# Spreading background steps, moving a DMA chain to GpSimd and re-ordering waits in a two-block transformer kernel

## Chip, cores and metric

One core of a Trainium2 chip runs the whole program. The metric is device microseconds of one execution, the median of several runs. The trace comes from one profiled execution, whose own time stands beside its span below.

## What is computed

Two model blocks of two layers each act on a sequence of 256 positions with 1024 channels. Layer 0 mixes by a state-space model (SSM) and by attention with 8 heads, layer 1 by a conformer convolution, layer 2 by latent attention (MLA) that also sees a context sequence, layer 3 by a Hyena convolution. After each mixer stands a gated feed-forward part. Each layer's norm is scaled and shifted by a modulation vector, a product of a conditioning vector with a large matrix. Cut to what matters:

```
for layer in range(DEPTH):                        # first block, DEPTH = 2
    mod = cs @ mod_w[layer] + mod_b[layer]        # 1024 x 6144
    sh1, sc1, g1, sh2, sc2, g2 = split(mod, 6)
    h = modulate(rms_norm(x, norm_g[layer, 0]), sh1, sc1)
    y = concat(s5_mixer(...), moba_attention(...)) @ ab_w_out   # layer 0
    y = conformer_conv(h, ...)                                  # layer 1
    x = x + g1 * y
    h = modulate(rms_norm(x, norm_g[layer, 1]), sh2, sc2)
    x = x + g2 * conv_ffn(h, ...)
x = rms_norm(x, final_g)
# second block: the same frame; layer 0 needs hc = modulate(rmsnorm(ctx), csh1, csc1)
# for the keys and values of the context, layer 1 is the Hyena mixer
```

## The kernel before

Activations lie channel by channel: eight tiles of 128 channels by 256 positions. All weights are float32 and are read once. A linear layer goes over blocks of 128 output channels (`linear`). For each block, `wsplit` takes a 512 KB load slot (`room`), loads the weights from the SP queue, lets ACT round them into `hi` (line 412) and DVE subtract to get `lo` (line 413); then `mm3` issues three matmuls per 128 input channels (lines 434 to 436), 24 for a block of 1024 inputs. The load slots are five tiles of the pool `raw`; in some stages `more` adds a second pool `raw2`, and `room` then takes the two pools in turn. `raw2` lies on memory that the stage before has used.

The language's planner orders each engine's instructions by a simulated time. `issue_after(ins)` in the program makes the instructions traced in it follow `ins` if they are on the same engine.

Modulation vectors are made in two ways beside the main work. `modulation` (lines 520 to 561) multiplies on PE, with the matrix as the moving operand: it loads four 512 KB tiles for each 512 outputs and yields after every second load; the products go into tile `mo`. `dotted_with` (line 498) makes 128 outputs per unit on DVE: GpSimd's queue loads 512 KB into `mraw` (line 504), and one DVE instruction (line 506) multiplies and sums. `later` and `also` put such work into lists, and `tick`, called after each block of `linear`, advances them: a counter `done` or `dotted` grows by one per block, and as often as it exceeds the step length, a step is issued. `need(layer)` issues all that is left up to a layer. `pace` sets the step length of the DVE units. The counters keep what they have when a list is empty (`done`) or when the pace changes (`dotted`).

A norm's scale is not known when the next stage begins. `Front` starts the first blocks of the next linear layer on unscaled data (`zh`, `zl`), twelve of them without a tick, while `stats` sums squares on PE, runs a Newton chain for the reciprocal root on DVE (`rsqrt`, lines 628 to 639) and spreads the result with two matmuls (`spread`, line 644). `stats2` does this twice in a row, for a norm behind a norm.

The SSM's lag kernels are built in `ssm_params`: a table `ktab` goes to DRAM (`kd`, line 992), and eight loads bring it back shifted (`kmat`, line 996). `ssm_out` (line 1073) uses `kmat` in its first matmuls (line 1089). `layer_ab` calls it after the first of four pairs of attention heads. In layer 1's feed-forward part `ffn1`, the function `context` runs between the last pair of gate and up blocks and the down blocks: it loads the context, norms it (`ctx_operand`) and makes its keys and values (`kv_latent`). In `layer_mla`, `positions` multiplies the rotary part `pe` of the keys (line 1423).

Of the kernel before, what the change touches and what calls it, by code (L numbers as in the profile page):

```python
# [11 lines left out]
F32 = mybir.dt.float32  # L12
# [265 lines left out]
class Front:  # L278
# [40 lines left out]

    def block(self, ps, wh, wl, evac):  # L320
# [4 lines left out]
        if self.n == 0 or self.n == self.spread:  # L325
            with net.tc.issue_after(net.last.ins):
                r = next(self.stats)
            if self.n:
                self.r = net.zp.tile([P, T], F32, name="zr")
                nc.scalar.activation(self.r, r, AF.Copy)  # L330
# [17 lines left out]
class Net:  # L348
    newton = 3

    def __init__(self, ctx, tc, d, where, dbg=None):
# [4 lines left out]
        self.turn = 0  # L356
# [81 lines left out]
    def linear(self, w, blocks, xh, xl, evac, n=T, acc=None):  # L438
# [132 lines left out]
    def pace(self, every):  # L571

        self.every = every
# [11 lines left out]
    def tick(self, n=1.0):  # L585
# [42 lines left out]
    def rsqrt(self, v):  # L628

        nc = self.nc  # L630
        y = self.t([P, 2], "ny")
        u = self.t([P, 2], "nu")
# [33 lines left out]
    def stats2(self, sq, sq2, r1):  # L666
# [101 lines left out]
    def down(self, w, hi, lo, evac, every=1.0):  # L768

        self.pace(every)  # L770
        self.linear(w, range(Front.late), hi, lo, evac)
# [4 lines left out]
    def ffn1(self, l, x, hi, lo, g2, sq, sq2=None, pool=None, mid=None, front=None):  # L776
        nc, d = self.nc, self.d
        with self.tc.tile_pool(name=f"ffn{l}", bufs=1, reuse_waits="tile") as fp:
# [19 lines left out]
            for j in range(FC):  # L798
                pair(j)
            if mid:  # L800
                mid()
            self.down(d[f"down{l}"], ah, al, self.residual(x, g2, sq, None, sq2, pool, front))
# [48 lines left out]
    def ssm_params(self, sp, spt):  # L851
# [265 lines left out]
    def layer_ab(self, x, hi, lo, g1, sq, sp, u2, vals, front):  # L1117
        nc, d = self.nc, self.d
        v = nc.vector
        with self.tc.tile_pool(name="ab", bufs=1, reuse_waits="tile") as ap, self.banks(mm=2, s=2, ax=1, o=1):  # L1120
# [23 lines left out]
            for c in range(4):  # L1144
# [3 lines left out]
                if c == 0:  # L1148
                    yc, yh, yl = self.ssm_out(sp, ap, u2)
# [230 lines left out]
    def ctx_operand(self, cxp, ch, cl, gc, sh):  # L1380
        nc, d = self.nc, self.d
        cx = []
        for k in range(0, DC, 4):
            raw = self.room().rearrange("p (k t) -> p k t", t=T)
            nc.sync.dma_start(raw, d["ctxT"][:, k : k + 4, :])
            cx += [raw[:, i, :] for i in range(4)]
        cq = []
        for k in range(DC):
            self.sumsq(cq, cx[k], k, DC, pool=cxp)
        r = self.rstd(cq, D)  # L1390
        for k in range(DC):
            t = self.t([P, T], "n2", pool=cxp)
            nc.vector.scalar_tensor_tensor(t, cx[k], gc[:, k : k + 1], r, op0=ALU.mult, op1=ALU.mult)
            nc.scalar.activation(ch[:, k, :], t, AF.Identity, bias=sh[:, k : k + 1])
            nc.vector.scalar_tensor_tensor(cl[:, k, :], t, sh[:, k : k + 1], ch[:, k, :].bitcast(F32),
                                           op0=ALU.add, op1=ALU.subtract)

    def layer_mla(self, x, hi, lo, g1, sq, ckh, ckl, pe, final, front):
        nc, d = self.nc, self.d
        v = nc.vector  # L1400
        with self.tc.tile_pool(name="mla", bufs=1, reuse_waits="tile") as mp:
# [18 lines left out]
            def positions(half):  # L1420
                s = slice(half * T, half * T + T)
                kp = self.ring("o")[:, s]
                nc.tensor.matmul(kp, self.rsum[:64, :], pe[:64, s], start=True, stop=True)
# [115 lines left out]
    def hy_filters(self, fp, hp, H):  # L1539
# [37 lines left out]
        for n in range(2):  # L1577
            ps = self.ax()
            nc.tensor.matmul(ps[:, :T], w, cur, start=True, stop=True)
            a = fp.tile([P, T], F32, name="fa", tag="fa")  # L1580
# [116 lines left out]
    def run(self, out):  # L1697
# [15 lines left out]
        with self.tc.tile_pool(name="sp", bufs=1, reuse_waits="tile") as sp:  # L1713
# [76 lines left out]
        next(cm)  # L1790
# [6 lines left out]
        self.ffn1(0, x, f, None, six(0, 5), sq, mid=mid, front=f2)  # L1797
# [3 lines left out]
        self.later(5, self.modulation(2, range(4), ("c_2", "c_ctx_2"), (mods[2], modc)), 5.0)  # L1801
# [12 lines left out]
        with self.tc.tile_pool(name="lat", bufs=1, reuse_waits="tile") as lat:  # L1814
# [8 lines left out]
            with self.tc.tile_pool(name="cx", bufs=1, reuse_waits="tile") as cxp:  # L1823

                def context():
                    ch = self.zp.tile([P, DC, T], F32R, name="ch", tag="zh")
# [88 lines left out]
```

## Time and profile before

| | us |
|---|---|
| median of 3 runs | 1523.81 (1521.16 to 1525.88) |
| the profiled execution's own time | 1522.47 |
| its span, first to last instruction | 1520.7 |
| PE busy | 1379.3 (91%) |
| PE weight loads busy | 1249.7 (82%) |
| DVE busy | 1195.9 (79%) |
| ACT busy | 839.3 (55%) |
| mean granted TensorE clock | 0.959 |

PE is TensorE's matmuls, DVE the vector engine, ACT the scalar engine, POOL GpSimd, SP the engine that issues most DMAs. L412 is line 412 of the kernel. A matmul that the clock grants half speed counts as busy for twice as long, so busy time is not all work. Times within the span count from its start.

### The profile page before, as it was taken

Reading aid. Unit: us, or ns where it says so; the run is one execution under the profiler, and the core shown is the slowest. Engines: PE = TensorE matmul, PEld = TensorE weight load, DVE = VectorE, ACT = ScalarE, POOL = GpSimd, SP = SyncE. Lnnn points to the kernel's source line nnn. Section 1 sums busy time; section 2 is a strip of 40 time slices with the busy share of each in tenths; the row PEclk is TensorE's granted clock in tenths of the full one; section 3 lists DMA queues with packets and bytes.
Section 4 is the critical chain, followed back from the end, with each engine's and each line's share of the span. In section 5 each row is a group of like instructions: output and inputs, shape, how many; then the busy total and the mean of one; then the engine's idle time right before and its main releaser. Section 6 shows DMA issues by size and latency. Waiting matters only on the chain.

```text
span 1520.7 us, 28172 instructions
## 1 busy us (share of the span) xinstructions
PE 1379.3 (91%) x10686; PEld 1249.7 (82%) x10686; DVE 1195.9 (79%) x2428; ACT 839.3 (55%) x1562; POOL 125.1 (8%) x166
## 2 busy tenths in 40 slices
PE   6969879999988689989987998989999999889997
PEld 3638779999973689989986877989998678889997
DVE  7958869978674678787968876899886979799954
ACT  5416466554452467554545765766545654676642
POOL 1000100101000000000100651000010000000000
PEclk9969989999999799998988999999999999999998
DMA  9476766878669246775835243467695664556651
GB/s 363 167 160 211 240 233 212 286 250 303 237 231 364 76 156 187 237 240 187 321 90 186 84 140 124 143 200 249 213 353 181 247 237 138 164 167 211 205 171 39
DMA packets 96214, 311.89 MB, mean 205 GB/s; under 512 B 14533, under 2 KB 18222, under 8 KB 95950
## 3 DMA queue, kind: packets, MB, share of 16 engines
q1 hardware_dynamic: 77054, 244.01, 48.7%
q0 software_dynamic: 17856, 65.02, 13.1%
q8 instruction: 84, 1.38, 0.4%
q10 hardware_dynamic: 1168, 1.06, 0.3%
q14 instruction: 52, 0.43, 0.1%
HBM read 308.73 MB, written 1.32 MB: 204 GB/s over the span
## 4 chain that ended last, share of the span: by engine, by line
PE 59%; issue 27%; DVE 6%; DMA 4%; ACT 2%; POOL 1%; SPq 0%; DVEq 0%; POOLq 0%; ACTq 0%
PE mm L434 16%; PE mm L436 16%; PE mm L435 16%; DVE lo L413 2%; PE o L1512 1%; POOL mraw L504 1%; DMA raw<-gate 1%; PE mo L532 1%; ACT hi L412 1%; PE ax L1612 1%; DMA kmat<-kd 1%; DVE mraw L506 1%; PE sx L1496 0%; PE s L434 0%; PE ax L1496 0%
## 5 line engine op out<-in xcount | busy, mean ns | idle before, releaser
L412 ACT ACTIVATE hi<-raw 128x1024 fp32r<-128x1024 f32 (+3 forms) x402 | 403.7, 1008 | 406.0 <-PE mm L435 285.3
L413 DVE TENSOR_TENSOR lo<-raw,hi 128x1024 fp32r<-128x1024 f32 (+3 forms) x402 | 465.3, 1161 | 167.0 <-ACT hi L412 161.8
L434 PE MATMUL mm<-hh,hi 128*128 128x256 f32 x1472 | 416.9, 287 | 16.4 <-DVE e L758 5.6
L436 PE MATMUL mm<-hh,lo 128*128 128x256 f32 x1472 | 415.5, 283 | 3.0 <-DVE lo L413 3.0
L435 PE MATMUL mm<-hl,hi 128*128 128x256 f32 x1472 | 414.9, 283 | 0.5 <-DVE hl L712 0.5
L434 PEld LDWEIGHTS mm<-hh,hi 128*128 128x128 f32 x1472 | 278.2, 190 | 26.0 <-issue 6.9
L435 PEld LDWEIGHTS mm<-hl,hi 128*128 128x128 f32 x1472 | 280.0, 190 | 5.1 <-DVE hl L712 2.0
L436 PEld LDWEIGHTS mm<-hh,lo 128*128 128x128 f32 x1472 | 279.8, 190 | 4.7 <-DVE lo L413 3.8
L434 PE MATMUL mm<-ah,hi 128*128 128x256 f32 x704 | 200.8, 286 | 1.5 <-ACT hi L412 1.5
L436 PE MATMUL mm<-ah,lo 128*128 128x256 f32 x704 | 198.6, 284 | 3.8 <-DVE lo L413 3.8
L435 PE MATMUL mm<-al,hi 128*128 128x256 f32 x704 | 198.3, 282 | 0.0
L434 PE MATMUL mm<-zh,hi 128*128 128x258 f32 x608 | 176.4, 295 | 20.6 <-ACT hi L412 10.9
L436 PE MATMUL mm<-zh,lo 128*128 128x258 f32 x608 | 176.2, 291 | 2.3 <-DVE lo L413 2.3
L435 PE MATMUL mm<-zl,hi 128*128 128x258 f32 x608 | 176.2, 291 | 0.0
L504 POOL DMA_DIRECT2D mraw<-modt x124 | 65.7, 530 | 1230.1 <-DVE mraw L506 1111.1
L506 DVE SCALAR_TENSOR_TENSOR mraw<-mraw,crow 128x1024 f32<-128x1024 f32 x124 | 149.9, 1219 | 6.3 <-DMA mraw<-modt 6.2
L434 PEld LDWEIGHTS mm<-zh,hi 128*128 128x128 f32 x608 | 118.9, 197 | 23.2 <-ACT hi L412 11.7
L436 PEld LDWEIGHTS mm<-ah,lo 128*128 128x128 f32 x704 | 132.6, 189 | 4.8 <-DVE lo L413 4.4
L434 PEld LDWEIGHTS mm<-ah,hi 128*128 128x128 f32 x704 | 133.3, 189 | 3.1 <-ACT hi L412 1.9
L435 PEld LDWEIGHTS mm<-al,hi 128*128 128x128 f32 x704 | 133.4, 190 | 1.0 <-issue 1.0
L436 PEld LDWEIGHTS mm<-zh,lo 128*128 128x128 f32 x608 | 119.7, 197 | 2.9 <-DVE lo L413 2.9
L435 PEld LDWEIGHTS mm<-zl,hi 128*128 128x128 f32 x608 | 120.6, 199 | 0.0
(416 smaller groups left out, 2076.4 us busy)
## 6 DMA issues: line engine op xcount, KB each, us to landing
raw<-up SPq DMA_DIRECT2D x132, 512.0 KB, 4.0
mraw<-modt POOLq DMA_DIRECT2D x124, 512.0 KB, 5.2
raw<-down SPq DMA_DIRECT2D x64, 512.0 KB, 4.6
raw<-mod SPq DMA_DIRECT2D x60, 512.0 KB, 6.2
raw<-gate SPq DMA_DIRECT2D x44, 512.0 KB, 4.7
raw<-down SPq DMA_DIRECT2D x32, 384.0 KB, 3.5
raw<-hy_in SPq DMA_DIRECT2D x24, 512.0 KB, 6.8
raw<-cm_in SPq DMA_DIRECT2D x16, 512.0 KB, 5.5
```

The source lines that it names most:

```text
L412: nc.scalar.activation(hi, src, AF.Copy)
L413: return nc.vector.tensor_tensor(lo, src, hi.bitcast(F32), op=ALU.subtract)
L434: nc.tensor.matmul(out, wh, xh, start=start, stop=False)
L435: nc.tensor.matmul(out, wh, xl, start=False, stop=False)
L436: self.last = nc.tensor.matmul(out, wl, xh, start=False, stop=stop)
L504: nc.gpsimd.dma_start(w, self.d[f"modt{layer}"][u])
L506: nc.vector.scalar_tensor_tensor(w, w, 1.0, row, op0=ALU.mult, op1=ALU.mult, accum_out=out[:, u : u + 1]))
L532: nc.tensor.matmul(acc[g * 32 : g * 32 + 32, :], wt, src, start=(g not in begun), stop=last)
L1512: nc.tensor.matmul(o[i * 64 : i * 64 + 64], vals[:, k, c : c + 64], pt[i][:, k, :], start=(k == 0), stop=(k == 3))
L1612: nc.tensor.matmul(ps, m[:, k, m0 : m0 + P], src[:, k, s], start=(k == 0), stop=(k == 1))
```

## The change

It has these parts:

- `tick` sets `done` to zero when no modulation step is left, and `pace` sets `dotted` to zero; in layer 1 of the first block the step length of the modulation on PE for layer 2 goes from 5.0 to 2.0. In layer 0 one more block of 512 outputs is made on PE (`range(4, 7)`), and DVE makes 12 units where it made 16, at pace 1.0 where it was 1.2.
- `kd` and `kmat` are issued from GpSimd's queue, and `ssm_out` follows the second pair of heads, behind the last matmul traced.
- The context's norm runs in three steps, before pairs 15, 17 and 18 of the feed-forward part, and the steps of `kv_latent` run behind the down blocks.
- `stats2` computes both reciprocal roots in one chain on four columns.
- The first five loads after `more` take slots of `raw`. The convolution filter's loads are issued before pair 8 and no longer at the stage's start.
- In `Front`, the weight splits of blocks 3 and 4 follow the Newton chain on DVE. `positions` follows the last matmul traced. One Hyena tile comes from another pool.

```diff
+    def guard(self):
+        return self.net.tc.issue_after(self.chain.ins) if self.n in (3, 4) else nullcontext()
...
     def room(self):
+        if self.hold:
+            self.hold -= 1
+            return self.raw.tile([P, 1024], F32, name="raw")
...
                 if front.first():
-                    front.block(ps, *self.wsplit(w[mb]), partial(evac, mb))
+                    with front.guard():
+                        wh, wl = self.wsplit(w[mb])
+                    front.block(ps, wh, wl, partial(evac, mb))
...
     def pace(self, every):
-        self.every = every
+        self.every, self.dotted = every, 0.0
...
             self.step()
+        if not self.pending:
+            self.done = 0.0
...
-        v1 = self.t([P, 2], "nv")
-        v.tensor_scalar(v1, st[:, 0:2], 1.0 / D, EPS, op0=ALU.mult, op1=ALU.add)
-        y1 = self.rsqrt(v1)
-        v2 = self.t([P, 2], "nv")
-        v.tensor_tensor(v2, y1, y1, op=ALU.mult)
-        v.tensor_tensor(v2, v2, st[:, 2:4], op=ALU.mult)
-        v.tensor_scalar(v2, v2, 1.0 / D, EPS, op0=ALU.mult, op1=ALU.add)
-        y2 = self.rsqrt(v2)
-        v.tensor_tensor(y2, y2, y1, op=ALU.mult)
+        a = self.t([P, 4], "nv4")
+        v.tensor_scalar(a[:, :2], st[:, 0:2], 1.0 / D, EPS, op0=ALU.mult, op1=ALU.add)
+        v.tensor_scalar(a[:, 2:], st[:, 2:4], 1.0 / D, None, op0=ALU.mult)
+        v.scalar_tensor_tensor(a[:, 2:], a[:, :2], EPS, a[:, 2:], op0=ALU.mult, op1=ALU.add)
+        y = self.rsqrt(a, 4)
+        y1, y2 = y[:, :2], y[:, 2:]
...
     def more(self, bufs):
             self.raws.append((p, "raw2"))
+            self.hold = 5
...
+    def down(self, w, hi, lo, evac, every=1.0, then=None):
+        for m in range(Front.late):
+            self.linear(w, [m], hi, lo, evac)
+            if then:
+                self.behind(then)
...
-            nc.sync.dma_start(kd[:, q, :, :].rearrange("s h m -> h s m"), kt[q * 32 : q * 32 + 16, :, :])
+            nc.gpsimd.dma_start(kd[:, q, :, :].rearrange("s h m -> h s m"), kt[q * 32 : q * 32 + 16, :, :])
...
-            nc.sync.dma_start(kmat[j * 16 : j * 16 + 16, :, j * 16 :],
+            nc.gpsimd.dma_start(kmat[j * 16 : j * 16 + 16, :, j * 16 :],
...
-                if c == 0:
-                    yc, yh, yl = self.ssm_out(sp, ap, u2)
+                if c == 1:
+                    with self.tc.issue_after(self.last.ins):
+                        yc, yh, yl = self.ssm_out(sp, ap, u2)
...
-            self.later(0, self.modulation(0, range(4, 6), cs, mods[:1]), 1.5)
+            self.later(0, self.modulation(0, range(4, 7), cs, mods[:1]), 1.5)
-            self.pace(1.2)
-            self.also(1, 0, 24, 40, row, mods[0])
+            self.pace(1.0)
+            self.also(1, 0, 28, 40, row, mods[0])
...
-        next(cm)
-        self.ffn1(0, x, f, None, six(0, 5), sq, mid=mid, front=f2)
+        self.ffn1(0, x, f, None, six(0, 5), sq, mid=mid, front=f2, at={8: lambda: next(cm)})
...
-        self.later(5, self.modulation(2, range(4), ("c_2", "c_ctx_2"), (mods[2], modc)), 5.0)
+        self.later(5, self.modulation(2, range(4), ("c_2", "c_ctx_2"), (mods[2], modc)), 2.0)
...
-                    self.ffn1(1, x, f, None, six(1, 5), sq, sq2, lat, context, f2)
+                    self.ffn1(1, x, f, None, six(1, 5), sq, sq2, lat, context, f2, {j: lambda: next(ctx) for j in (15, 17, 18)}, latent)
```

## Rows read from the trace of the kernel before

**Rows 1.** The page: span, and PE's busy time

```profile
span 1520.7 us, 28172 instructions
PE 1379.3 (91%) x10686; PEld 1249.7 (82%) x10686; DVE 1195.9 (79%) x2428; ACT 839.3 (55%) x1562; POOL 125.1 (8%) x166
```

**Rows 2.** PE's waits by releaser: us in total, times, longest

```profile
PE sx L644 <- DVE ny L638: 18.6, 6, 6.2
PE sx L1089 <- DMA kmat<-kd: 15.0, 1, 15.0
PE mm L434 <- ACT hi L412: 14.3, 8, 9.8
...
PE o L1423 <- DVE pe L1370: 4.5, 1, 4.5
...
PE sx L644 <- DVE ny L681: 3.4, 1, 3.4
```

**Rows 3.** Busy time by stretch: length, engines, granted clock, DMA share, GB/s

```profile
85.70:100.60 14.90, 0.00 (x0) 0.00 (x0) 8.73 (x33) 0.00 (x0) 0.00 (x0) 0.57 1.13 131
100.70:111.80 11.10, 11.10 (x113) 6.32 (x114) 3.03 (x3) 3.66 (x4) 0.00 (x0) 0.50 0.83 295
85.70:186.60 100.90, 83.18 (x728) 67.44 (x728) 73.93 (x177) 45.36 (x97) 7.40 (x14) 0.88 0.77 217
...
186.60:207.80 21.20, 9.43 (x59) 8.72 (x59) 10.56 (x21) 8.31 (x16) 2.36 (x4) 0.76 0.79 284
442.60:476.50 33.90, 25.45 (x125) 5.03 (x124) 5.81 (x19) 5.48 (x15) 1.05 (x2) 1.00 0.99 384
...
678.00:692.00 14.00, 6.65 (x28) 6.25 (x29) 10.01 (x31) 6.47 (x12) 0.00 (x0) 0.64 0.41 141
...
778.70:791.00 12.30, 6.41 (x28) 6.15 (x29) 8.22 (x23) 5.46 (x15) 0.00 (x0) 0.59 0.12 39
805.80:818.40 12.60, 6.25 (x22) 5.01 (x23) 8.81 (x37) 4.08 (x11) 0.53 (x1) 0.59 0.48 181
...
600.00:680.00 80.00, 78.00 (x659) 77.91 (x657) 64.45 (x110) 47.61 (x78) 4.22 (x8) 1.00 0.75 241
```

**Rows 4.** SP's queue in order of time, 60 to 100 us: start, length, issue

```profile
62.67 0.33 SPq L542 DMA_DIRECT2D raw<-mod  x1
82.59 1.77 SPq L992 DMA_DIRECT2D kd<-ktab  x4
87.15 8.25 SPq L996 DMA_DIRECT2D kmat<-kd  x8
...
97.64 0.35 SPq L425 DMA_DIRECT2D raw<-ab_in  x1
```

**Rows 5.** SP's queue in order of time, 170 to 212 us

```profile
171.34 10.49 SPq L425 DMA_DIRECT2D raw<-up  x5
...
187.47 0.43 SPq L425 DMA_DIRECT2D raw<-gate  x1
```

**Rows 6.** PE in order of time, 442 to 453 us: modulation products

```profile
442.57 4.50 PE L532 MATMUL mo<-raw,cs 128*32 128x512 f32 x40
...
448.74 1.05 PE L532 MATMUL mo<-raw,cs 128*32 128x512 f32 x4 [1.30 <-DMA raw<-mod]
```

**Rows 7.** DVE in order of time, 551 to 560 us: a Newton chain

```profile
551.61 0.16 DVE L653 TENSOR_SCALAR nv<-sx 128x2 f32<-128x2 f32 x1 [2.44 <-PE sx L624]
...
557.06 1.22 DVE L413 TENSOR_TENSOR lo<-raw,hi 128x1024 fp32r<-128x1024 f32 x1 [0.30 <-ACT hi L412]
558.21 0.15 DVE L638 SCALAR_TENSOR_TENSOR ny<-nu,ny 128x2 f32<-128x2 f32 x1
```

**Rows 8.** DVE in order of time, 799 to 811 us: a modulation unit

```profile
807.93 1.23 DVE L506 SCALAR_TENSOR_TENSOR mraw<-mraw,crow 128x1024 f32<-128x1024 f32 x1 [1.78 <-DMA mraw<-modt]
```

**Rows 9.** The page's DMA issues: count, KB each, median us to landing

```profile
mraw<-modt POOLq DMA_DIRECT2D x124, 512.0 KB, 5.2
...
raw<-gate SPq DMA_DIRECT2D x44, 512.0 KB, 4.7
```

More of the change, by code (lines that the diff above doesn't have):

```diff
@@ L327, in block @@
                 r = next(self.stats)
+                if self.n == 0:
+                    self.chain = net.chain
             if self.n:
@@ L355, in __init__ @@
         self.dbg = dbg or {}
-        self.turn = 0
+        self.turn = self.hold = 0
         self.ahead = False
@@ L626, in sums, with rsqrt @@
         return last
-    def rsqrt(self, v):
+    def rsqrt(self, v, n=2):
         nc = self.nc
-        y = self.t([P, 2], "ny")
-        u = self.t([P, 2], "nu")
+        y, u = (self.t([P, n], nm + (str(n) if n > 2 else "")) for nm in ("ny", "nu"))
         nc.vector.tensor_scalar(u.bitcast(I32), v.bitcast(I32), 1, None, op0=ALU.logical_shift_right)
@@ L764, in more, with ffn1 @@
             self.raws.append((p, "raw2"))
+            self.hold = 5
             yield
             self.raws.pop()
-    def down(self, w, hi, lo, evac, every=1.0):
+    def down(self, w, hi, lo, evac, every=1.0, then=None):
         self.pace(every)
-        self.linear(w, range(Front.late), hi, lo, evac)
+        for m in range(Front.late):
+            self.linear(w, [m], hi, lo, evac)
+            if then:
+                self.behind(then)
         self.pace(1000.0)
         self.linear(w, range(Front.late, DC), hi, lo, evac)
-    def ffn1(self, l, x, hi, lo, g2, sq, sq2=None, pool=None, mid=None, front=None):
+    def ffn1(self, l, x, hi, lo, g2, sq, sq2=None, pool=None, mid=None, front=None, at={}, then=None):
         nc, d = self.nc, self.d
@@ L798, in ffn1 @@
             for j in range(FC):
+                if j in at:
+                    at[j]()
                 pair(j)
@@ L801, in ffn1 @@
                 mid()
-            self.down(d[f"down{l}"], ah, al, self.residual(x, g2, sq, None, sq2, pool, front))
+            self.down(d[f"down{l}"], ah, al, self.residual(x, g2, sq, None, sq2, pool, front), then=then)
     def ffn2(self, l, x, hi, lo, g2, sq, mid, front=None):
@@ L1378, in kv_latent, with ctx_operand @@
         yield
-    def ctx_operand(self, cxp, ch, cl, gc, sh):
+    def ctx_operand(self, cxp, ch, cl, modc):
         nc, d = self.nc, self.d
+        self.need(5)
+        g = self.gain("a2c", modc[:, 8:16], self.par("norm_mix_g_2", 0, 8))
+        sh = modc[:, 0:8]
         cx = []
@@ L1386, in ctx_operand @@
             cx += [raw[:, i, :] for i in range(4)]
+        yield
         cq = []
@@ L1389, in ctx_operand @@
             self.sumsq(cq, cx[k], k, DC, pool=cxp)
-        r = self.rstd(cq, D)
+        stats = self.stats(cq, D)
+        self.behind(stats)
+        yield
+        with self.tc.issue_after(self.last.ins):
+            r = next(stats)
         for k in range(DC):
             t = self.t([P, T], "n2", pool=cxp)
-            nc.vector.scalar_tensor_tensor(t, cx[k], gc[:, k : k + 1], r, op0=ALU.mult, op1=ALU.mult)
+            nc.vector.scalar_tensor_tensor(t, cx[k], g[:, k : k + 1], r, op0=ALU.mult, op1=ALU.mult)
             nc.scalar.activation(ch[:, k, :], t, AF.Identity, bias=sh[:, k : k + 1])
@@ L1422, in positions @@
                 kp = self.ring("o")[:, s]
-                nc.tensor.matmul(kp, self.rsum[:64, :], pe[:64, s], start=True, stop=True)
+                with self.tc.issue_after(self.last.ins):
+                    nc.tensor.matmul(kp, self.rsum[:64, :], pe[:64, s], start=True, stop=True)
                 for i in range(4):
@@ L1579, in hy_filters @@
             nc.tensor.matmul(ps[:, :T], w, cur, start=True, stop=True)
-            a = fp.tile([P, T], F32, name="fa", tag="fa")
+            a = self.t([P, T], "e")
             v.tensor_scalar(a, ps[:, :T], self.par("hy_f", 2 * n), self.par("hy_f", 2 * n + 1), op0=ALU.add, op1=ALU.mult)
@@ L1823, in run @@
             with self.tc.tile_pool(name="cx", bufs=1, reuse_waits="tile") as cxp:
+                ch, cl = (self.zp.tile([P, DC, T], F32R, name=n, tag=t) for n, t in (("ch", "zh"), ("cl", "zl")))
+                ctx = self.ctx_operand(cxp, ch, cl, modc)
+                latent = self.kv_latent(ch, cl, ckh, ckl, pe, 0, kv0, cxp, self.ax)
                 def context():
-                    ch = self.zp.tile([P, DC, T], F32R, name="ch", tag="zh")
-                    cl = self.zp.tile([P, DC, T], F32R, name="cl", tag="zl")
                     self.need(6)
@@ L1831, in context @@
                     self.also(7, 2, 24, 40, row2[0], mods[2])
-                    gc = self.gain("a2c", modc[:, 8:16], self.par("norm_mix_g_2", 0, 8))
-                    self.ctx_operand(cxp, ch, cl, gc, modc[:, 0:8])
-                    for _ in self.kv_latent(ch, cl, ckh, ckl, pe, 0, kv0, cxp, self.ax):
-                        pass
+                    next(latent)
+                    self.behind(latent)
                 def gain():
```

1 line of the change is left out of this document (added).

## The prediction

> **What bounds the kernel now.** First the page: of a span of 1520.7 us PE is busy for 1379.3 [rows 1], so at most 141 us can be won by closing PE's idle time, plus what PE loses at half clock. Second PE's waits [rows 2]: the reader is to see that a few long waits carry much of it, one of 15.0 us on the lag kernels, one of 9.8 on a weight split, six on Newton chains, 18.6 in all. Third the stretches around those waits and around every place where DMA is near its top [rows 3]; there the reader sees idle PE and the granted clock: after the 15 us wait PE works 11.1 us at 0.50, the lower of its two levels (1.2 GHz), so a wait costs its own length and then half of the work behind it. In the long feed-forward stretches PE is busy for 78.0 of 80 us [rows 3]; nothing is to be won there, and whatever the change adds to PE there is paid in full.
>
> **Part A, lag kernels and state-space output.** SP's queue shows the cause [rows 4]: after a load at 62.67 it issues nothing until `kd` at 82.59, then eight `kmat` loads at 87.15, and the attention weights behind them only at 97.64. PE stands from 85.7 to 100.6 and then works 11.1 us at half clock: 14.9 + 5.6 = 20.5 us is the most that can go. The edit takes twelve issues from SP, so the weights come early and PE has the next query and key blocks to do. What is late next: DVE, busy for 73.9 of the stage's 100.9 us, less four units of 1.23 [rows 8], 69; and PE, 83.2 less 5.6 of slow clock, plus the added modulation block, four loads at 0.45 (below), 79.4. Both fit in 80 us, but PE now has less to put beside the first heads' softmax, because `ssm_out` comes a pair later. How long twelve small-row DMAs take on GpSimd no row shows. On SP the eight issues took 8.25 us and ended with the landing at 100.6; for equal loads of 512 KB GpSimd's take 5.2 and SP's 4.7 [rows 9]. The bounds are a gain of 20.5 and none; nearest is the wait's own row, and I take **13**. Behind them on GpSimd stand only `mraw` loads; three of these lie in their slots already, so DVE's first three units don't wait.
>
> The Trainium skill, SBUF — State Buffer, section "SBUF: two separate sides", says against this part that GpSimd cannot write descriptors for its DMAs while DVE runs an instruction in a mode with two ports. In the idle stretch DVE is busy for 8.73 of 14.9 us [rows 3], so by that rule, at most, `kmat` lands 8.7 us later and the gain falls to some 4; no row shows a GpSimd issue held in this way.
>
> **Part B, first feed-forward stage.** Before the stage ends SP loads five up tiles, and the first gate tile only at 187.47 [rows 5], since slots alternate and `raw2` becomes free with the stage. PE is busy for 9.43 of 21.2 us, at a clock of 0.76 [rows 3]: 11.8 idle and some 2 at half clock. With five held slots gate and up tiles of blocks 0 to 4 are there in time, five blocks of 24 matmuls; 659 in 80 us of the full stretch [rows 3] make 0.121 each, so five blocks are 14.5 us, an estimate, three times a load's 4.7 us [rows 9], and that covers the second pool's first landings. The four units fewer and the pace of 1.0 also take units and 512 KB loads off the stage's end, and the filter's loads move to pair 8, where PE is full and DMA is not. What is left is the last residual and its scaled copy on DVE and ACT, about 2 us. Bounds 3 and 13.7; I take **11**.
>
> **Part C, the burst in the convolution layer.** `done` grew during the whole feed-forward part, so the first tick issues all 14 steps at once: 12 + 16 = 28 loads. From 442.6 to 476.5 DMA is at 0.99 and PE busy for 25.45 of 33.9 us [rows 3]. Where the loads had landed, 40 rows, which are ten loads, took 4.50 us, 0.45 a load; where PE followed the loads, one took 1.05 [rows 6], as fewer products run side by side. Set to zero, the counter gives two loads per step: one step in the four blocks that tick, three in `fill` calls where PE is idle in any case, two under the output blocks, eight in the next feed-forward part. Six loads are hidden, 22 cost 0.45 to 0.53, 10 to 11.7 us. Of the stretch stay some 2 us of transposes. 33.9 - 2 - 11 = 21; I take **20**, bounds 10 and 22. The price is elsewhere: eight steps, 8.4 MB, come into the feed-forward part at 241 GB/s [rows 3]. In the 50 to 59 us that the steps take there, 12.1 + 8.4 = 20.5 MB need 53 us at the burst's 384 GB/s. That just fits: **1 us lost**, bounds 0 and 8. In the Hyena layer the same reset spreads 16 loads; PE is full there, so 0, with 3 either way.
>
> **Part D, the context.** From 678 to 692 PE is busy for 6.65 us at a clock of 0.64 [rows 3]: 7.4 idle, with the 6.2 us wait for a Newton chain [rows 2] in it, and up to 3.3 of half clock. The chain, the scaling and the context's blocks now lie beside the last pairs, where DVE is busy for 64.45 of 80 us; of the 10.0 us that DVE works in the first stretch most move there, which finds room in seven pairs (41 us) but not in one. I take **8**, bounds 2 and 10.7.
>
> **Part E, guard.** (18.6 - 6.2) / 5 = 2.5 us is each other wait on a Newton chain; three of the five are at a `Front`. The chain of 12 short instructions takes from 551.61 to 558.36, with four `lo` of 1.2 us in between [rows 7]. Two of them now come behind it; the chain ends some 2.3 earlier. But block 3 may then wait for its own `lo`, 1.2. I take 1.5 at each of three places, **4.5**, bounds 7.5 gained and 3.7 lost.
>
> **Part F, latent attention.** `stats2` saves 13 of 27 chain instructions, 13 x 0.16 = 2.1 [rows 7], and its guard two `lo`: the 3.4 us wait [rows 2] goes. Later PE waits 4.5 for `pe` [rows 2], because DVE stands behind units whose loads have not landed [rows 8]: `dotted` came in full from the stage before, and the reset ends that burst; besides, `positions` no longer overtakes the blocks before it. Both waits are followed by work at half clock, 0.59 over stretches with 6.41 and 6.25 busy [rows 3], up to 3.1 us each. 3.4 + 4.5 + 6.2 = 14.1 at most, none at least; I take **9**.
>
> **Sum.** 13 + 11 + 20 - 1 + 8 + 4.5 + 9 = 64.5. The profiled execution took 1522.5, 1.8 more than its span and 1.3 less than the median of 1523.8. 1522.5 - 64.5 = 1458; with the 1.3, **1459 us**.
>
> **Rivals.** (1) *A wait takes the place of the one removed*: `kmat` lands so late that PE, in order, stands at `ssm_out` as long as before. For it speaks that all small rows pass one issuing engine; against, that two more blocks of PE work and a softmax lie ahead of it. A is 0: 1472. (2) *The modulation loads meet DMA's limit* in the feed-forward part, 53 of at most 59 us: C gains 10 and costs 8: 1476. (3) *The change doesn't do what it says*: the planner keeps its simulated order, and since the edges bind one engine only, E and F bring nothing: 1459 + 13.5 = 1472.5. (4) *Slower*: the twelve DMAs crawl on GpSimd. The other parts gain 51.5; PE would have to stand at `ssm_out` for more than 14.9 + 51.5 = 66 us, that is `kmat` has to land after about 152 us, which is 69 us for twelve DMAs from 83 on, 5.8 each in a row. Then the units' loads behind them on GpSimd hold DVE too. From there it is slower than before, 1530 at 76 us of standing. Against it: a GpSimd load of 512 KB takes 5.2 us with its landing and several are in flight at a time.
>
> **How the numbers follow.** The forecast, 1440 to 1470, gets 0.53; (1) 0.15, (2) 0.13, (3) 0.11, (4) 0.04; a further 0.04 is for many parts at their low ends, 1500 to 1524. All upper bounds together, with 1 us for DMA left out, would give 1523.8 - 90 = 1434; I cut this at 1440, and on the other side go to 1492, past two rivals at once (1459 + 13 + 17 = 1489). A measurement of this kernel can tell 0.3%, 4.6 us, from no change. Faster: all of the forecast and of (1) to (3) and a little of the rest, 0.93; same 0.03; slower 0.04.
>
> **What would show it.** After the change PE's waits should have no entry for `kmat` above a few us, `ab_in` issues on SP should follow 63 us by some us, a gate tile should be issued before the stage's end, no stretch should have `mo` rows for more than 3 us in a row in the convolution layer, and the wait of 6.2 us, that of 3.4 and that of 4.5 should be gone. DMA in the second feed-forward part should rise to 300 GB/s or more with PE still full. The prediction is wrong if PE waits in that part for weights, if `ssm_out`'s first matmul waits over 10 us, or if the removed waits come back at the same places under another releaser.

## The result and the profile after

The changed kernel takes **1453.8 us** (median of 4 runs, 1450.3 to 1456.3), beside 1524.2 for the kernel before: a ratio of 0.954, with a 95% interval of 0.951 to 0.956, so 70 us are gone. The forecast was 1459, its range 1440 to 1492. The total is right; several of its terms are not, and that they cancel is luck, as the rest shows.

The page of the changed kernel: the span, and the engines' busy time.

```profile
span 1452.8 us, 28167 instructions
PE 1360.5 (94%) x10702; PEld 1239.5 (85%) x10702; DVE 1184.8 (82%) x2407; ACT 840.0 (58%) x1562; POOL 130.9 (9%) x174
```

PE's busy time fell by 19 us against [rows 1], and the span by 68: 49 us of the gain are idle time of PE. The mean granted clock rose from 0.959 to 0.973, so that less of the busy time is work at half clock. PE's waits by releaser (total, times, longest) show what is left.

```profile
PE mo L543 <- DVE s_den L923: 9.9, 1, 9.9
PE sx L656 <- DVE ny L650: 6.7, 3, 2.5
PE mm L443 <- ACT hi L418: 6.4, 5, 3.6
PE mm L443 <- DVE qk L419: 5.1, 1, 5.1
PE mm L445 <- DVE lo L419: 5.0, 9, 1.1
PE mm L443 <- DVE n L344: 4.3, 3, 3.3
...
PE o L1221 <- ACT pt L1214: 3.5, 2, 3.2
PE ax L1212 <- DVE ssb L1209: 3.4, 1, 3.4
PE mm L443 <- DVE at L419: 3.3, 1, 3.3
```

Against [rows 2] the wait on `kmat` is gone and the waits on Newton chains (`ny`) fell from 18.6 to 6.7. Those on `n`, the evacuation of a `Front`'s first block, fell to 4.3 from this row of before:

```profile
PE mm L434 <- DVE n L338: 9.5, 6, 2.5
```

New are four waits of 3.2 to 5.1 us, on `qk`, `at`, `pt` and `ssb`: all stand in the attention stage, where the wait on `kmat` stood, and their longest ones add up to 15.0 us, as much as that wait.

Where the time went is read from stages. Each `Front` starts with a matmul on `zh`; the times from one such first matmul to the next, in us of the profiled execution, are these (rows that begin with "before +" are the kernel before with one edit; those between "changed" and these are the changed kernel with one edit taken out):

| kernel | to first Front | ffn 1 | conv | ffn 2 | latent attn. | ffn 3 | Hyena | ffn 4 | span |
|---|---|---|---|---|---|---|---|---|---|
| before | 196.4 | 202.5 | 143.6 | 222.1 | 183.8 | 203.1 | 154.0 | 215.3 | 1520.7 |
| changed | 191.1 | 198.5 | 112.6 | 217.9 | 178.0 | 193.6 | 153.5 | 207.6 | 1452.8 |
| no guard | 190.2 | 199.3 | 121.3 | 215.4 | 175.6 | 197.3 | 156.9 | 211.8 | 1467.8 |
| burst back | 193.4 | 199.7 | 146.6 | 209.2 | 175.6 | 195.0 | 155.9 | 209.1 | 1484.5 |
| lag edit out | 180.9 | 198.0 | 112.0 | 215.2 | 177.9 | 194.5 | 154.3 | 208.4 | 1441.1 |
| place of `ssm_out` back | 183.8 | 199.0 | 113.5 | 216.6 | 171.1 | 194.0 | 153.9 | 206.1 | 1438.0 |
| no held slots | 196.2 | 200.4 | 112.0 | 213.1 | 172.3 | 194.2 | 152.8 | 207.7 | 1448.8 |
| no extra block | 198.0 | 199.3 | 111.9 | 214.9 | 177.9 | 193.8 | 152.6 | 206.7 | 1455.2 |
| context at once | 191.6 | 197.2 | 111.9 | 221.3 | 174.2 | 193.7 | 153.2 | 208.3 | 1451.4 |
| counter kept | 189.4 | 197.3 | 113.1 | 216.6 | 178.3 | 193.7 | 154.2 | 207.7 | 1450.4 |
| two chains | 191.8 | 198.7 | 112.6 | 216.1 | 180.7 | 192.5 | 153.5 | 207.6 | 1453.4 |
| before + no burst | 196.2 | 205.3 | 118.1 | 230.2 | 178.9 | 203.5 | 155.1 | 211.0 | 1498.2 |
| before + lag edit | 200.7 | 202.6 | 142.8 | 221.0 | 182.6 | 198.1 | 156.7 | 211.0 | 1515.5 |
| best | 185.3 | 197.6 | 112.0 | 211.4 | 175.9 | 193.7 | 153.6 | 207.1 | 1436.5 |

Two things are to be seen. The convolution layer alone gave 31.0 of the 68 us, the two last feed-forward stages 17.2, and the stages up to the first `Front`, where the prediction put most of the 24 us of its parts A and B, gave 5.3 (B's stretch runs 11 us past it, and the first feed-forward stage gave 4.0). And stages that an edit doesn't touch change too: latent attention takes 171 to 178 us in kernels whose code for it is the same as in the changed one. The planner sets each engine's order for the whole program, and one edit in the first layer can alter it in far stages. The traces show this: PE's order in latent attention is the same in the changed kernel and with the lag edit out (178.0 and 177.9 us), and another one without held slots and with `ssm_out`'s place taken back (172.3 and 171.1). So a difference of 5 to 7 us in a far stage, and in the total, says nothing of the edit's own place.

### The profile page after: what moved, and what is told of

Same layout as the page of the kernel before. It is cut to its first block, busy times and chain, and to the rows that moved or that the text cites. A ratio compares the mean times of both kernels' runs of the same rounds, so it can differ in the third digit from the quotient of the medians.

```text
span 1452.8 us, 28167 instructions
## 1 busy us (share of the span) xinstructions
PE 1360.5 (94%) x10702; PEld 1239.5 (85%) x10702; DVE 1184.8 (82%) x2407; ACT 840.0 (58%) x1562; POOL 130.9 (9%) x174
## 5 line engine op out<-in xcount | busy, mean ns | idle before, releaser
L443 PE MATMUL mm<-ah,hi 128*128 128x256 f32 x704 | 199.0, 283 | 3.6 <-ACT hi L418 3.6
L443 PE MATMUL mm<-zh,hi 128*128 128x258 f32 x608 | 172.9, 287 | 6.5 <-DVE n L344 3.5
L517 DVE SCALAR_TENSOR_TENSOR mraw<-mraw,crow 128x1024 f32<-128x1024 f32 x120 | 144.7, 1217 | 3.1 <-DMA mraw<-modt 2.9
L444 PEld LDWEIGHTS mm<-zl,hi 128*128 128x128 f32 x608 | 117.1, 193 | 0.2 <-DVE zl L304 0.2
```

The costliest lines, as they stand in the source:

```text
L443: nc.tensor.matmul(out, wh, xh, start=start, stop=False)
L444: nc.tensor.matmul(out, wh, xl, start=False, stop=False)
L517: nc.vector.scalar_tensor_tensor(w, w, 1.0, row, op0=ALU.mult, op1=ALU.mult, accum_out=out[:, u : u + 1]))
```

## Experiments

Each kernel is the changed one with one edit taken out, unless said otherwise; each was timed against runs of the kernel before on its own chip, so ratios are compared. The changed kernel's is 0.9538 (0.9513 to 0.9564); 0.001 is 1.5 us.

**The guard taken out.**

```diff
-        return self.net.tc.issue_after(self.chain.ins) if self.n in (3, 4) else nullcontext()
+        return nullcontext()
```

> The changed kernel with the guard alone taken out: the weight splits of blocks 3 and 4 of every Front may stand inside the Newton chain again. The prediction's step gives 4.5 us (1.5 at three Fronts), so 1458. The rival reads the seven Front runs of the two traces: from the first matmul on zh to the last they went from 41.1 to 36.2, 40.7 to 36.8, 43.6 to 38.4, 33.0 to 28.6, 40.2 to 36.2, 42.1 to 38.9 and 42.5 to 40.0 us, 28 us in all, because the waits on the evacuation of the first block's result and the half clock behind each wait count too, and not only the waits on the chain. By it the guard's loss costs 15 to 25 us, 1469 to 1479, and the Front runs are longer by 2 to 4 us each.

Measured: 1468.6 us, 0.9629 (0.9605 to 0.9654): 14 us lost, just under what the rival gave and three times the prediction's 4.5. DVE in order of time at the `Front` before the Hyena layer, without the guard:

```profile
1105.67 0.16 DVE L665 TENSOR_SCALAR nv<-sx 128x2 f32<-128x2 f32 x1 [3.68 <-PE sx L637]
...
1107.61 1.22 DVE L419 TENSOR_TENSOR lo<-raw,hi 128x1024 fp32r<-128x1024 f32 x1
...
1113.54 1.23 DVE L419 TENSOR_TENSOR lo<-raw,hi 128x1024 fp32r<-128x1024 f32 x1 [0.65 <-ACT hi L418]
1114.68 0.15 DVE L650 SCALAR_TENSOR_TENSOR ny<-nu,ny 128x2 f32<-128x2 f32 x1
```

The chain takes 9.2 us, with weight splits in it; with the guard the same chain takes 4.2 (1098.13 to 1102.35). What that costs PE stands in its waits from 191 to 1290 us, without the guard and then with it:

```profile
PE mm L443 <- DVE n L344: 12.9, 8, 3.3
PE sx L656 <- DVE ny L650: 8.1, 4, 2.5
```

```profile
PE mm L443 <- DVE n L344: 4.3, 3, 3.3
PE sx L656 <- DVE ny L650: 4.2, 2, 2.5
```

12.5 us of waits come back, most of them on `n`, which needs the chain's result. They stand at six of the seven `Front`s; at latent attention the wait of 3.3 us on `n` stands with the guard too. Then the clock: PE's busy time and granted clock (columns: stretch, length, PE busy, clock, DMA share, GB/s) at this `Front` without the guard, and the same place in the changed kernel.

```profile
1112.50:1125.00 12.50, 9.12 (x52) 0.73 0.30 88
```

```profile
1106.00:1118.00 12.00, 12.00 (x101) 1.00 0.70 227
```

Behind a wait of 2.45 us on the chain and one of 0.93 on `n` PE runs at its lower level (1.2 GHz) for 6.8 us, as the mean clock of 0.73 over 12.5 us gives. Over the whole kernel PE's idle time is 7.2 us longer without the guard, since some other waits are shorter, and its busy time 7.8. So about half of what the guard is worth is waits; most of the rest is half clock.

**The burst put back.**

```diff
-        if not self.pending:
-            self.done = 0.0
...
-        self.later(5, self.modulation(2, range(4), ("c_2", "c_ctx_2"), (mods[2], modc)), 2.0)
+        self.later(5, self.modulation(2, range(4), ("c_2", "c_ctx_2"), (mods[2], modc)), 5.0)
```

> The changed kernel with the counter of PE's modulation steps not set to zero, and a step length of 5.0 for layer 2's: all steps come at once in the convolution layer again. The prediction's step gives 20 us less 1 for DMA in the feed-forward part: 1473. The rival: the convolution layer went from 143.6 to 112.6 us, and if all of that is the burst's, less the 6.4 us that twelve loads now cost in the feed-forward part, it is 25 us, 1478. If other parts (the guard, the two waits on the conv) carry more than 4 us of the layer's gain, it is nearer 1470.

Measured: 1487.9 us, 0.9767 (0.9722 to 0.9812): 34 us lost, above both figures. The convolution layer is longer by 34.0 and the second feed-forward stage shorter by 8.7 in the table: 25.3 at the edit's own places, near the rival's 25. The other 6 us of the longer span are spread over the other stages; only the Hyena layer's share, 2.4, stands where the edit acts too. PE's modulation products in the layer, with the burst (some of its rows) and then in the changed kernel:

```profile
438.92 3.56 PE L543 MATMUL mo<-raw,cs 128*32 128x512 f32 x22
...
445.74 1.05 PE L543 MATMUL mo<-raw,cs 128*32 128x512 f32 x4 [0.19 <-DMA raw<-mod]
446.96 1.05 PE L543 MATMUL mo<-raw,cs 128*32 128x512 f32 x4 [0.17 <-DMA raw<-mod]
```

```profile
435.36 1.07 PE L543 MATMUL mo<-raw,cs 128*32 128x512 f32 x8
```

The burst lasts from 433.4 to 465.5, 32.1 us; spread, two loads cost 1.07 together. (One row in the changed kernel's layer, of three steps at 449.8, is 3.75 us long, over the 3 us that the prediction had named as its sign.) Behind the burst stand waits that the prediction didn't price, since it ended its stretch with the burst: 6.2 us on `zh` (1.9 in the changed kernel) and 4.4 on `cmY` (0.7):

```profile
PE mm L443 <- ACT zh L303: 6.2, 1, 6.2
PE mm L1354 <- ACT cmY L1347: 4.4, 1, 4.4
```

**The lag edit taken out.** The twelve loads are on SP again and `ssm_out` follows the first pair.

```diff
-            nc.gpsimd.dma_start(kd[...])          # and kmat
+            nc.sync.dma_start(kd[...])
...
-                if c == 1:
-                    with self.tc.issue_after(self.last.ins):
-                        yc, yh, yl = self.ssm_out(sp, ap, u2)
+                if c == 0:
+                    yc, yh, yl = self.ssm_out(sp, ap, u2)
```

> The changed kernel with the lag kernels' twelve loads back on SP's queue and ssm_out after the first pair of heads. The prediction's step gives 13 us lost, 1467, with the wait of 15 us on kmat back. The rival reads the changed kernel's trace: the stage that ended at 186.6 now ends at 191.1, with 12 us of PE waits at 88.6, 103.1, 143.7 and 147.7, so the wait on kmat only uncovered DVE's state recursion (80 to 98 us) and the last pair's softmax; by it this kernel is within 4 us of the changed one, 1450 to 1458, and may be faster.

Measured: 1441.4 us, 0.9461 (0.9427 to 0.9494): **faster** than the changed kernel by 12. The prediction has the wrong sign, and the wait on `kmat` does not come back:

```profile
103.62 0.42 PE L1106 MATMUL sx<-kmat,u 128*32 128x128 f32 x8 [0.30 <-DMA kmat<-kd]
```

PE waits 0.3 us there, with the loads on SP. In the changed kernel this work comes at 120.3.

**Which half of the lag edit.** Only the place of `ssm_out` is taken back; the loads stay on GpSimd.

```diff
-                if c == 1:
-                    with self.tc.issue_after(self.last.ins):
-                        yc, yh, yl = self.ssm_out(sp, ap, u2)
+                if c == 0:
+                    yc, yh, yl = self.ssm_out(sp, ap, u2)
```

> The changed kernel with ssm_out after the first pair of heads and no issue order for it, the lag kernels' loads staying on GpSimd's queue. It tells which half of the edit costs the 12 us that the kernel with both halves taken out gained (1441.4). If it is the place of ssm_out, because the last pair's softmax then has no output blocks of PE beside it, this kernel takes 1440 to 1445. If it is GpSimd's queue, whose unit loads now stand behind the twelve small loads, 1450 to 1455.

Measured: 1441.4 us, 0.9444 (0.9417 to 0.9471). In the total it is the place: the two kernels can't be told apart. By stage the queue is not settled. The stages up to the first `Front` are 7.3 us shorter with the place alone taken back and 10.2 with both halves, so that SP's queue is 2.9 ahead there, and in latent attention, where neither edit acts, it is 6.8 behind; differences of this size come from the planner's order as well. In the changed kernel PE, in order of time, stands twice in the last pair's softmax:

```profile
143.03 0.65 PE L1221 MATMUL o<-pt,vals 128*64 128x256 f32 x2
146.84 0.86 PE L1221 MATMUL o<-pt,vals 128*64 128x256 f32 x6 [3.17 <-ACT pt L1214]
151.08 0.87 PE L1212 MATMUL ax<-ident,ssb 128*128 128x128 f32 x3 [3.37 <-DVE ssb L1209]
151.60 0.77 PE L443 MATMUL mm<-yhl,hi 128*128 128x256 f32 x2
```

The first block behind `ssm_out`, on `yhl`, comes at 151.6, after these waits. With `ssm_out` earlier it comes at 143.6 and lies beside the softmax:

```profile
143.62 0.79 PE L443 MATMUL mm<-yhl,hi 128*128 128x256 f32 x2
```

**The lag edit alone, on the kernel before.**

```diff
-            nc.sync.dma_start(kd[...])            # and kmat
+            nc.gpsimd.dma_start(kd[...])
...
-                if c == 0:
-                    yc, yh, yl = self.ssm_out(sp, ap, u2)
+                if c == 1:
+                    with self.tc.issue_after(self.last.ins):
+                        yc, yh, yl = self.ssm_out(sp, ap, u2)
```

> The kernel before with the lag kernels' loads on GpSimd's queue and ssm_out after the second pair of heads, and nothing else changed. The prediction's step gives 13 us gained, 1511. The rival: the wait on kmat goes, and DVE's state recursion and the last pair's softmax, which it covered, stand in its place, 10 to 12 us with half clock behind; then 0 to 6 us are gained, 1518 to 1524.

Measured: 1517.3 us, 0.9943 (0.9923 to 0.9963): 9 us gained, between the two. But not at its place: the stage up to the first `Front` is 4.3 us longer, and 9.3 come from the third and fourth feed-forward stages, whose code the edit doesn't touch. There DVE's order is another one than before, while in the first two feed-forward stages, as long as before within 1.1 us, PE's and DVE's orders are unchanged: it is the planner's new order.

**The burst removed alone, on the kernel before.**

```diff
             self.step()
+        if not self.pending:
+            self.done = 0.0
...
-        self.later(5, self.modulation(2, range(4), ("c_2", "c_ctx_2"), (mods[2], modc)), 5.0)
+        self.later(5, self.modulation(2, range(4), ("c_2", "c_ctx_2"), (mods[2], modc)), 2.0)
```

> The kernel before with one edit alone: the counter of PE's modulation steps is set to zero when no step is left, and layer 2's step length is 2.0. The prediction's step gives 19 us gained, 1505. The rival: taking this edit out of the changed kernel cost 34 us, and the edits of the prediction's parts A, B, D, E and F, taken out one by one, cost 14.7 for the guard and nearly nothing or less for the others, so that half of the gain of 70 us is in no part alone. By the rival this edit also moves ssm_out on PE, from behind the first query and key block to behind the third, since the ten modulation products no longer come in one row ahead of it: the wait of 15 us on kmat goes although the lag kernels are still on SP's queue. Then 34 + 13 to 20 us are gained, 1470 to 1477.

Measured: 1499.1 us, 0.9808 (0.9762 to 0.9854): 27 to 29 us gained, between the two again. The rival's mechanism is there: PE's first product with `kmat` stands three query and key blocks later in its order, and PE's waits from 77 to 197 us, the three longest, hold no `kmat`, with its loads on SP:

```profile
PE mm L434 <- ACT hi L412: 9.2, 1, 9.2
PE mm L434 <- DVE qk L413: 3.8, 1, 3.8
PE sx L1091 <- ACT ys L1096: 1.9, 1, 1.9
```

In the kernel before, a row of modulation products stood there at once (twenty matmuls in the trace, five loads), and the wait behind it:

```profile
82.90 2.77 PE L532 MATMUL mo<-raw,cs 128*32 128x512 f32 x20
```

So the wait on `kmat` hung on this row as much as on SP. But the rival's gain is not: the stage ends at 187.1, where it ended at 186.6, and the 9.2 us wait stands there still. DVE and PE from 77.5 to the stage's end (columns as in [rows 3]):

```profile
77.50:187.10 109.60, 98.84 (x884) 79.64 (x882) 80.59 (x203) 46.05 (x100) 7.40 (x14) 0.88 0.68 192
```

The mean clock is 0.88: three stretches, 27 us, at the lower level, in which PE is busy for 24.1. Before it was one of 24 us, from within the long wait on, in which PE was busy for 11.1. The wait of 15 us was worth nothing by itself: up to the first `Front` PE's idle time falls from 44.2 to 37.4 us, and its busy time rises from 152.2 to 158.8 with as many matmuls. What the shorter waits gave, slower work took: 13 us more at half clock in these stretches are 6.5 us of lost work. Why the clock fell there no run singles out.

**The held slots taken out.**

```diff
-            self.hold = 5
```

> The changed kernel with the five held slots taken out: after a second pool opens, loads take the two pools in turn from the first one on, as before. The convolution filter's loads stay before pair 8 and the units at pace 1.0. The prediction's step gives up to 11 us lost for this first feed-forward stage, 1465, with a wait of about 10 us before its first block. The rival reads the changed trace: its first gate load is issued at 175.6 us, 15 us before the stage ends, and the second pool opens in three more stages of the kernel, so the slots count there too and the loss is 14 to 20 us. A second rival: the units and the filter's loads did it, and the loss is under 4.

Measured: 1448.9 us, 0.9479 (0.9446 to 0.9512): not slower, and by its interval just faster. The first `Front` starts 5.1 us later, but the wait there is 2.4 us of it, not 10: two causes had made it. The second feed-forward stage and latent attention are shorter by 4.8 and 5.7 without the slots; in latent attention PE's order is another one too, so that no run shows this to be the slots' own cost.

**The extra modulation block taken out.**

```diff
-            self.later(0, self.modulation(0, range(4, 7), cs, mods[:1]), 1.5)
+            self.later(0, self.modulation(0, range(4, 6), cs, mods[:1]), 1.5)
-            self.pace(1.0)
-            self.also(1, 0, 28, 40, row, mods[0])
+            self.pace(1.2)
+            self.also(1, 0, 24, 40, row, mods[0])
```

> The changed kernel with two blocks of modulation outputs on PE in layer 0 and sixteen units at pace 1.2, as before, in place of three blocks and twelve units. If the extra block only costs its PE time, four loads of 0.53 us, this kernel is 2 us faster in the attention stage and pays up to 1 us of units in the first feed-forward part: 1452 to 1454. The rival: the block's loads also hold slots, and the next query and key load, issued at 99.21 only, lands at 102.2 while PE waits; then it is 4 to 6 us faster in the attention stage. A third: the four units cost the first feed-forward stage its clean start, and this kernel is 2 to 5 us slower.

Measured: 1453.2 us, 0.9536 (0.951 to 0.9562), the same. At its place it is not the same: the first `Front` starts 6.9 us later, with the gate tiles loaded early. PE's wait there, and DVE before it:

```profile
PE mm L443 <- ACT zh L303: 7.5, 1, 7.5
```

```profile
185.96 1.22 DVE L517 SCALAR_TENSOR_TENSOR mraw<-mraw,crow 128x1024 f32<-128x1024 f32 x1
...
188.57 1.22 DVE L517 SCALAR_TENSOR_TENSOR mraw<-mraw,crow 128x1024 f32<-128x1024 f32 x1
190.11 1.23 DVE L517 SCALAR_TENSOR_TENSOR mraw<-mraw,crow 128x1024 f32<-128x1024 f32 x1 [0.32 <-DMA mraw<-modt]
...
192.79 0.48 DVE L753 SCALAR_TENSOR_TENSOR x<-mm,mod,x 128x256 f32<-128x256 f32 x1
194.44 1.23 DVE L517 SCALAR_TENSOR_TENSOR mraw<-mraw,crow 128x1024 f32<-128x1024 f32 x1 [1.18 <-DMA mraw<-modt]
...
197.07 0.17 DVE L519 TENSOR_TENSOR mod<-mod,p 128x16 f32<-128x16 f32 x1
```

The last residual is done at 193.3, but the `Front` also needs `mod`, the units' own result, for its scale, and the last unit starts only at 194.44 after a wait for its load. In the changed kernel `mod` is ready at 180.2, before at 190.2. So the 9.8 us wait of [rows 2] had two causes side by side, a late gate tile and late units: with either one left, PE waits. With units early but no held slots it is 2.4 us, with slots but late units 7.5, with neither cause none.

**The context at one place again.**

```diff
-                    self.ffn1(..., context, f2, {j: lambda: next(ctx) for j in (15, 17, 18)}, latent)
+                    self.ffn1(..., context, f2, {}, None)      # context() runs ctx and latent to their ends
```

> The changed kernel with the context's norm and its latent product all at one place again, between the last pair and the down blocks of layer 1's feed-forward part. The prediction's step gives 8 us lost, 1462, with a wait on a Newton chain of about 6 us near 650. The rival: that part of the program, feed-forward and down, went from 222.1 to 217.9 us while it took in 6.4 us of modulation products and a Front shorter by 5, so that the context is worth 4.2 + 6.4 - 5 = 5.6; and a wait of 3.6 us on a weight split stands there now at 646.9. By it the loss is 3 to 6 us.

Measured: 1459.1 us, 0.9553 (0.9518 to 0.9588): 2 to 5 us, not told from none. In its stage 3.4 are lost: PE waits 6.5 us on the chain, and the 3.6 us wait on a weight split, which took its place in the changed kernel, is gone.

```profile
PE sx L656 <- DVE ny L650: 6.5, 1, 6.5
```

**The counter of the units kept at `pace`; and `stats2` in two chains.**

```diff
-        self.every, self.dotted = every, 0.0
+        self.every = every
```

> The changed kernel with the counter of DVE's units kept when the pace changes. The prediction has it in its part on latent attention only, as the 4.5 us wait and its half clock: 5 us lost, 1459. The rival: the two feed-forward parts of the second block went from 203.1 to 193.6 and from 215.3 to 207.6 us, 17.2 in all, of which the guard's removal gave back 3.7 and 4.1; the rest, 9.4, would then be the counter's, since before three units in a row stood in front of a weight split there (PE waited 2.8 and 2.15 us). By it 9 to 14 us are lost, 1463 to 1468.

Measured: 1451.7 us, 0.9501 (0.9467 to 0.9535): no loss, and the last feed-forward stages stay as they are. A wait of 3.9 us on a Newton chain stands in its latent attention, a stage as long as in the changed kernel.

```diff
-        y = self.rsqrt(a, 4)
-        y1, y2 = y[:, :2], y[:, 2:]
+        y1 = self.rsqrt(v1)
...
+        y2 = self.rsqrt(v2)
+        v.tensor_tensor(y2, y2, y1, op=ALU.mult)
```

> The changed kernel with the two reciprocal roots of latent attention's entry in two chains again. The prediction's step: the 3.4 us wait comes back, with up to 1.5 of half clock behind it, 3 to 5 us lost, 1457 to 1459. The rival: what ended that wait was the place of the splits in the chain and not its length, and since the guard has moved these, only the 2.1 us of the saved instructions count, less what lies beside PE's work: 0 to 2 us.

Measured: 1452.9 us, 0.9507 (0.9473 to 0.954): no loss in the total; latent attention, where this edit acts, is 2.7 us longer, though the 3.4 us wait does not come back.

**A better version**: the lag edit out, held slots in the first feed-forward stage only.

```diff
-            self.hold = 5
+            self.hold = 5 if bufs == 5 else 0
```

> The changed kernel without the parts that were found to cost: the lag kernels on SP's queue, ssm_out after the first pair, and held slots in the first feed-forward stage only. If the two savings add, 1453.8 - 12.4 - 4.9, and the held slots of the first stage (5 us of shorter wait there) stay: 1432 to 1437. If the held slots' cost elsewhere was an effect of the planner's order and not of the slots, 1440 to 1444.

Measured: 1438.2 us, 0.9422 (0.9395 to 0.945): 16 to 18 us faster than the changed kernel, between the two figures of its forecast. The 3 us against the kernel with the lag edit alone out can't be told from none.

## Why the prediction was right, and where it was not

| step | predicted gain | its removal cost | what decided |
|---|---|---|---|
| A, lag kernels | 13 | -12 (9 gained alone) | the place of `ssm_out` |
| B, first stage | 11 | slots -5 to -9, extra block and units 0 | two causes of one wait |
| C, burst | 20 - 1 | 34, 25 of it at its places (27 to 29 alone) | right, and waits behind it |
| D, context | 8 | 2 to 5 | a new wait of 3.6 us |
| E, guard | 4.5 | 14 | waits at six `Front`s, not three, and half clock behind most |
| F, latent attention | 9 | chain 0 (2.7 in its stage), counter 0 | open |

The mechanisms of C and E are right; A's sign is wrong. That the sum came within 6 us of the result is luck: A's error of 25 us stands against some 25 us more than forecast in C and E, and of the 28 us of B, D and F the removals bring back at most 5. The single effects don't add to 70 either: with those that the removals show, 34 + 14 + 3 - 12 - 5 = 34 us are accounted for. Pairs of causes, as at the first `Front`, hide from removals of one edit, and the planner's order shifts several us; how much of the other 36 us is due to each is not shown. Of the 17.2 us in the two last feed-forward stages the guard's removal brings back 7.9 and the counter's nothing; the lag edit alone gained 9.3 there, but its removal loses only 1.7. Two sums of the prediction are off by little: its upper bounds add up to 88.5 and not 90, and rival (4)'s 76 us of standing give 1533 and not 1530.

**A failed at its first step.** The prediction held SP's twelve issues for the cause and let the query and key blocks follow. Only one more did: SP's next `ab_in` issue, forecast some us after 63, stands at 71.58, and the one behind it ends the row at 93.4, as the slots were full, waiting for splits.

```profile
71.58 21.86 SPq L434 DMA_DIRECT2D raw<-ab_in  x2
```

DVE was late: the state recursion (`tx`, `X`) ran without a gap from 80.3 on. ACT had begun on that tile's `hi` at 84.48 and on `qk` at 85.45, but the split that frees a slot came at 91.88, and PE waited 5.13 us for the `qk` split behind it.

```profile
90.78 0.42 DVE L1076 TENSOR_TENSOR tx<-X,pr 128x64 f32<-128x64 f32 x2
...
91.88 1.21 DVE L419 TENSOR_TENSOR lo<-raw,hi 128x1024 fp32r<-128x1024 f32 x1
...
93.20 0.40 DVE L419 TENSOR_TENSOR qk<-mm,qk 128x256 fp32r<-128x256 f32 x1
```

The prediction summed DVE's busy time over the stage, 69 of 80 us, which says nothing of its order; rows of before showed the recursion only beside PE's long wait, where it was free. The sum of an engine's work does not show what is late next, its order does. This tells why the edit did not gain, not why it cost: with `ssm_out`'s place taken back, SP's row (71.92, 21.99 us) and the wait for `qk` (5.2) are the same. Rival (1), a wait in the place of the one removed, came near, though not on `kmat`: four waits in the stage of 15.0 us in all. The remark that `ssm_out` comes a pair later, with less beside the softmax, was the deciding point, and stood there at no price; it cost 12 us, 7.3 of them in this stage. "`ssm_out`'s first matmul waits over 10 us" was the sign named for a failure; it didn't wait at all, and the part failed in another way.

**The rule on descriptors, set against A.** GpSimd's queue in order of time, and the stretch of the eight `kmat` issues (columns as in [rows 3]):

```profile
90.03 4.97 POOL L1013 DMA_DIRECT2D kmat<-kd  x8 [3.45 <-DMA kd<-ktab]
```

```profile
90.03:95.00 4.97, 1.25 (x6) 1.28 (x7) 4.97 (x18) 0.00 (x0) 4.96 (x8) 0.84 0.82 118
```

DVE was busy for all 4.97 us and GpSimd issued eight loads in them, 0.62 each, back to back; its next two loads, of 512 KB each, took 0.57 and 0.55. No issue was held for the 4.97 us, nor for one of DVE's longer instructions (1.2). The Trainium skill, VectorE: DVE Perf Modes, section "Why `tensor_tensor` can't do 2×_2P or 4×", gives instructions with two tensor operands no such mode, and most of DVE's there are of that kind; this row agrees with that, and no run here tests the rule on other instructions. Rival (4), GpSimd at a crawl, is out.

**B** took the right stretch, and a gate tile is issued at 175.6, before the stage ends, as forecast; but it priced one cause of two; the prediction did name the units, at no price of their own, and where it left about 2 us for the last residual, the wait was 7.5 with late units. **C** was right in kind and size: two loads cost 1.07 in the new places, 0.53 each where 0.45 to 0.53 was taken, and of the 8.7 us that the second feed-forward stage pays, twelve loads are 6.4, which the sum held (it put eight steps there; six came, and eight, not six, in the convolution layer). DMA rose as forecast and PE stayed full (from 541 to 586 us), so rival (2) is out:

```profile
541.00:586.00 45.00, 44.62 (x364) 38.57 (x364) 33.31 (x57) 26.05 (x46) 1.58 (x3) 1.00 0.84 302
```

At its own places it was too small by 6 us, as it left out the 8 us of waits behind the burst. **D**'s wait went, and one of 3.6 us on a split of the down weights took its place, the kind of exchange that the prediction's bound of 2 allowed for. **E** counted three of the sites that [rows 2] lists under a chain and left out those listed under `n`, which wait for the same chain, and the clock behind most of them. Rival (3), the planner undoing it, is out for E. **F**'s waits of 3.4 and 4.5 us are gone from their releasers, but neither of the edits taken out alone brings a loss in the total; a wait of 3.3 us on `n` stands in the changed kernel at 734.5, where before 3.4 on the chain and 2.5 on `n` stood. For F, rival (3) may hold in part. The later `positions`, the filter's later loads and the Hyena tile's pool were not tried by themselves.

## What to carry to other kernels

A long wait of the bounding engine names what came last, not what the stage would cost without it; follow the order of the next engine through the freed stretch before pricing the gain. A wait can have two causes side by side, and then one edit alone shows nothing. Where a planner orders the whole program, compare stage by stage: a total can move by 9 us, as with the lag edit alone, for reasons far from the edit.

## What the runs showed of the hardware

Short waits can cost more than the list of waits shows: behind one of 2.45 us and one of 0.93, PE ran for 6.8 us at the lower clock, which lost it 3.4 more. Not each such wait does. Without the guard six of the seven `Front`s have 3.4 to 6.8 us at the lower clock behind their waits; at the first, a wait of 2.17 us is followed by a clock of 1.00 (205.4 to 212.0), and in the kernel before the same pair of 2.45 and 0.93 us, near 1167, has none either. So the granted clock behind a wait has to be read, not assumed.

And a stretch with little idle time can still be slow: 27 of 110 us at half clock with only 10.8 idle in the stage of the burst's removal alone. In the longest of its three slow stretches, 13.7 us from 116.1 on, PE was busy all the time.
